# The SSD decode step with state rows on partitions: outer product and output on TensorE, one pass each on GpSimd and VectorE

## The chip, the cores and the metric

One core of one Trainium2 chip. The metric is the device time in microseconds (us) of one execution; the time of a kernel is the median of its runs. Names of engines: PE is TensorE's matmuls, PEld its weight loads, DVE is VectorE, ACT is ScalarE, POOL is GpSimd, SP issues DMAs.

## What is computed

One inference step of a two-layer decoder trunk for 1024 prompt tokens and 8 decode tokens (8 sequences, one new token each). Layer 0 is a hybrid of gated DeltaNet and retention, layer 1 is a Mamba-2 SSD mixer; a squared-ReLU MLP stands behind each. The change is in the SSD mixer's decode step: for each of 8 sequences and 32 heads (4 groups of 8) with state size 128 and head size 64

```
S_new = S * exp(g) + outer(B, x * dt)      # [state 128, head 64]
y     = C^T S_new                          # per head, 64 values
```

where `g = dt * a`, B and C belong to the group, and `S_new` is an output of its own (4 x 8 tiles of 256 KB).

## The kernel before

Activations lie with features on the partitions and the 1032 tokens along the row. The projections are exact in float32: weights and activations are split into a high and a low part in the rounded type float32r, and each product is three matmuls of 344 columns (L150, L151, L152). A weight tile comes by DMA from SP into `raw`, is scaled by the norm's weights on GpSimd (L140), rounded by ScalarE to `whi` (L144), and its rest `wlo` is made by VectorE (L145).

The SSD mixer (`ssm_mixers`, L1441) goes through 4 groups. Each group has 6 projection tiles for x, B and C (evicted by VectorE at L1451 as `sxc`, then the convolution L408 to L413 and a SiLU at L420 and L421) and 4 gate tiles (`z`, L1476, L1487). `ssd_group` (L1569) handles the 1024 prompt tokens in 4 units of 2 chunks: transposes to tokens on partitions (L1598), `xdt` (L1600), scores `sc` (L1613), decay products (L1621) that need the banks which `xdt` and `sc` free, and then L1648 to L1666 for outputs and running state. The projection tiles of the next group and the gates of the one before are interleaved with it by generators, and so is the decode step:

```
            yield
            for _ in range(2 if u == 0 else 1):
                next(dec)
                yield
```

`ssd_decode` (L1674) first makes small tables and fetches states, then takes one pair of sequences per unit. The order in which each engine finally gets its instructions is set by the tile scheduler, which mixes these streams; each engine works through its list strictly in order. PSUM has three banks for projections (`pg`), three for small products (`pm`), taken in turn. Eight buffers of [128, 512] (`half`) are shared in turn by `xdt`, `xd2`, `yi`, and the decode step's `dS` and `dpr`.

In the decode step before, a state tile `dS` [128, 4 x 128] has the features (of head pairs) on the partitions and the 128 state rows along the row. TensorE only broadcasts rows of B and C over the partitions (L1718). Per state, ScalarE scales the four quarters by exp(g) (four L1725), VectorE adds B times x dt to each quarter (four L1727), GpSimd issues the store (L1728) and multiplies by C into `dpr` (L1730), and VectorE sums `dpr` over the state rows (L1731). The other mixer's decode step has states in the other layout and does products of states with two columns (L966), a scaling on GpSimd (L979), an outer product (L1021) and an add on VectorE (L981).

Of the kernel before, what the change touches and what calls it, by code (L numbers as in the profile page):

```python
# [10 lines left out]
F32 = mybir.dt.float32  # L11
# [8 lines left out]
T = 1032                     # 1024 prompt tokens, then 8 decode tokens  # L20
# [24 lines left out]
# order of the hybrid projection's m-tiles (first column of each)  # L45
# [14 lines left out]
# blocks of the output projections: the first packed column's k-tile, the mixer outputs  # L60
# [13 lines left out]
# columns of the retention's constants  # L74
# [9 lines left out]
class Pools:  # L84
    """A mixer's two pools: what the output projection's first block needs or reuses, and the rest."""
# [10 lines left out]
class Kern:  # L96
# [35 lines left out]
    def load_w(self, src, n, normw=None, lo_eng=None, dst=None, norm_eng=None):  # L132
        """src [128, n] of a packed weight unit -> exact float32r high and low parts."""
# [73 lines left out]
    def gemm_flush(self, src, parts, evict):  # L207
        """A block of k-tiles into all 8 m-tiles; src(m) the packed weights [128, 128 * k-tiles]."""
# [16 lines left out]
    def split_piece(self, m, n, src, ssq, tp):  # L225
        """src [128, 344] fp32 becomes the residual's piece (m, n); its squares go to ssq."""
# [16 lines left out]
    def rsqrt(self, out, src):  # L243
        """out = (src) ** -0.5 for a small tile."""
# [7 lines left out]
    def rstd_from(self):  # L252
        """rstd_bc[:, t] = (sum_p ssq[p, t] / 1024 + eps) ** -0.5 on every partition; ssq lies where rstd_bc does."""
# [42 lines left out]
    def load_x(self, gp):  # L296
        """The tokens, as exact parts; their rstd; and the narrow projection, not yet scaled by it."""
# [25 lines left out]
        def square(m):  # L323
            """x[m]'s squares; those of four tiles are added up."""
# [49 lines left out]
    def softplus(self, out, x, tp, tag, bufs=None):  # L374
        """log1p(exp(x)) = max(x, 0) + 2 atanh(u / (2 + u)), u = exp(-|x|)."""
# [40 lines left out]
    def silu2(self, x, scale, tp):  # L416
        """x (1 + tanh(scale x)) in place, in two halves."""
# [39 lines left out]
    def load_mixed(self, k, raw, hi, lo):  # L457
        """A spilled mixer output [128, 1024] and its decode columns, as exact parts."""
# [7 lines left out]
    def out_first(self, name, c0, parts, stage):  # L466
        """The first k-tiles of an output projection, with the residual, go to memory."""
# [12 lines left out]
    def hyb_mixers(self, gp):  # L480
# [34 lines left out]
        def ret(t, rr, vv, gg):  # L515
            for i in range(2):
# [3 lines left out]
                for q in range(4):          # the halves of each head's features change places  # L520
# [25 lines left out]
        def step():  # L546
            """Emits a sixth of a projection (and the end of the one before)."""
# [6 lines left out]
        def project(n):  # L554
            """Emits the projections up to tile n."""
# [6 lines left out]
        def weave(mix, need, rate):  # L562
            """Emits a mixer's pieces with `rate` sixths of a projection after each."""
# [16 lines left out]
        # the output projection's first block fills in while the last mixers finish  # L580
# [22 lines left out]
    def gdn_setup(self, gp, ba):  # L603
# [14 lines left out]
        gnh = gp.tile([P, 5], F32, name="gnh")     # norm weights of the gated outputs, halved  # L618
# [4 lines left out]
        # beta and decay: [8, T] -> token-major [128, 9, 8]  # L623
# [35 lines left out]
        # rows of the cumulated decay, as exact float32r parts stacked on the contraction  # L659
# [19 lines left out]
    def gdn_head(self, gp, h, feat, st):  # L679
# [21 lines left out]
        for bi in range(2):  # L701
# [33 lines left out]
            # decay, transposed: DT[j, c, i] = exp(min(G_i - G_j, mask))  # L735
# [1150 lines left out]
```

## Time and profile before

| | |
|---|---|
| runs | 3256.97, 3253.94, 3255.11 us; median 3255.11 |
| profiled execution, span of the trace | 3239.5 us (its time outside the span is not recorded; the median is 15.6 us above the span) |
| TensorE busy | 3086.4 us, 95% |
| VectorE, ScalarE, GpSimd busy | 1740.3 (54%), 896.2 (28%), 1241.3 (38%) |
| granted TensorE clock, mean | 0.960 of full speed |
| moved by DMA | 202.13 MB, mean 62 GB/s |

Busy times are shares of the whole span, so an engine that looks idle there can be the late one in a single stage. Matmuls overlap each other, so the mean length of one is larger than the step from one to the next; the step is read from counts in a stretch where TensorE never idles.

### The profile page before, as it was taken

To read this page: it belongs to the slowest core of one execution; us is meant where nothing else is said; L and a number is where in the kernel's file an instruction comes from. 1 tells how busy PE (TensorE), PEld (TensorE's weight loads), DVE (VectorE), ACT (ScalarE), POOL (GpSimd) and SP (SyncE) were. 2 spreads that over 40 slices of the span, in tenths; PEclk is the share of its full clock that TensorE was granted. 3 is DMA by queue.
4 is the path that set the end of the run, shared out by engine and by line. 5 is a ranking of instruction groups with operands and counts; after the bars stand their busy time and mean duration, and the time that the engine had idled before them with its cause. 6 is when DMAs were issued, how large, how long until landed. Compare 5 with 4: busy or idle time off the path is not lost. (4 is left out here: it accounts for less than half of the span.)

```text
span 3239.5 us, 49390 instructions
## 1 busy us (share of the span) xinstructions
PE 3086.4 (95%) x19566; PEld 2929.6 (90%) x19566; DVE 1740.3 (54%) x3201; ACT 896.2 (28%) x1828; POOL 1241.3 (38%) x1234
## 2 busy tenths in 40 slices
PE   7989998989999999999999999999899999999998
PEld 6888888879999999999987788887899999999998
DVE  7664667464333333337886785967635333333334
ACT  3222221223111111114444444354213111111112
POOL 4232324155333323225355555444625332332324
PEclk9899999889999999999998898998899999999999
DMA  3011103142111111111111111222431111111112
GB/s 123 20 47 54 47 26 112 55 168 64 46 46 47 49 46 46 48 48 40 55 56 58 69 62 43 82 69 79 157 140 43 46 47 49 46 46 50 46 46 72
DMA packets 102326, 202.13 MB, mean 62 GB/s; under 512 B 12624, under 2 KB 27728, under 8 KB 102096
## 3 DMA queue, kind: packets, MB, share of 16 engines
q1 hardware_dynamic: 94800, 173.82, 16.7%
q0 software_dynamic: 7296, 25.17, 2.0%
q8 instruction: 154, 2.52, 0.3%
q14 instruction: 76, 0.62, 0.1%
HBM read 157.94 MB, written 38.89 MB: 61 GB/s over the span
## 5 line engine op out<-in xcount | busy, mean ns | idle before, releaser
L150 PE MATMUL pg<-xh,whi 128*128 128x344 f32 x3072 | 1020.7, 332 | 10.2 <-DVE sxc L1451 6.5
L152 PE MATMUL pg<-xh,wlo 128*128 128x344 f32 x3072 | 1012.9, 330 | 2.8 <-DVE wlo L145 2.8
L151 PE MATMUL pg<-xl,whi 128*128 128x344 f32 x3072 | 1009.0, 328 | 0.0
L150 PEld LDWEIGHTS pg<-xh,whi 128*128 128x128 f32 x3072 | 593.0, 193 | 27.7 <-issue 8.8
L152 PEld LDWEIGHTS pg<-xh,wlo 128*128 128x128 f32 x3072 | 592.8, 193 | 12.7 <-issue 5.2
L144 ACT CAST whi<-raw 128x512 fp32r<-128x512 f32 (+2 forms) x443 | 271.0, 612 | 1191.5 <-PE pg L151 723.9
L151 PEld LDWEIGHTS pg<-xl,whi 128*128 128x128 f32 x3072 | 592.3, 193 | 8.8 <-issue 5.8
L140 POOL TENSOR_TENSOR raw<-raw,vec 128x512 f32<-128x512 f32 x264 | 300.7, 1139 | 589.9 <-DMA raw<-w 339.7
L151 PE MATMUL pg<-alo,whi 128*128 128x344 f32 (+2 forms) x1476 | 472.4, 320 | 0.0
L152 PE MATMUL pg<-ahi,wlo 128*128 128x344 f32 (+2 forms) x1476 | 472.3, 320 | 0.0
L150 PE MATMUL pg<-ahi,whi 128*128 128x344 f32 (+2 forms) x1476 | 471.6, 319 | 0.0
L1236 DVE TENSOR_TENSOR acc<-acc,pg 128x344 f32<-128x344 f32 x360 | 182.8, 511 | 385.4 <-PE pg L152 385.4
L145 POOL TENSOR_TENSOR wlo<-raw,whi 128x512 fp32r<-128x512 f32 (+2 forms) x179 | 223.7, 1251 | 327.7 <-ACT whi L144 326.6
L145 DVE TENSOR_TENSOR wlo<-raw,whi 128x512 fp32r<-128x512 f32 x264 | 209.6, 794 | 193.3 <-ACT whi L144 172.2
L1227 POOL TENSOR_TENSOR r<-r 128x344 f32<-128x344 f32 x192 | 145.9, 760 | 387.6 <-ACT ahi L1226 338.5
L152 PEld LDWEIGHTS pg<-ahi,wlo 128*128 128x128 f32 x1476 | 277.6, 188 | 0.0
L150 PEld LDWEIGHTS pg<-ahi,whi 128*128 128x128 f32 x1476 | 277.5, 188 | 0.0
L151 PEld LDWEIGHTS pg<-alo,whi 128*128 128x128 f32 x1476 | 277.3, 188 | 0.0
L1228 DVE TENSOR_TENSOR alo<-r,ahi 128x344 fp32r<-128x344 f32 x192 | 135.6, 707 | 253.8 <-POOL r L1227 253.8
L1226 ACT ACTIVATE ahi<-r 128x344 fp32r<-128x344 f32 x192 | 94.5, 492 | 338.5 <-DVE r L1225 338.5
L1225 DVE SCALAR_TENSOR_TENSOR r<-pg,rstd_bc 128x344 f32<-128x344 f32 x186 | 94.8, 510 | 76.9 <-PE pg L152 75.6
L150 PE MATMUL pg<-mhi,whi 128*128 128x344 f32 x408 | 131.3, 322 | 4.1 <-DVE acc L1342 4.1
(534 smaller groups left out, 4422.9 us busy)
## 6 DMA issues: line engine op xcount, KB each, us to landing
raw<-w SPq DMA_DIRECT2D x256, 256.0 KB, 2.6
raw<-wis SPq DMA_DIRECT2D x80, 256.0 KB, 2.6
raw<-wih SPq DMA_DIRECT2D x56, 256.0 KB, 2.6
mraw<-spill SPq DMA_DIRECT2D x17, 512.0 KB, 4.1
accd<-ost SPq DMA_DIRECT2D x48, 172.0 KB, 2.1
acc<-accd SPq DMA_DIRECT2D x16, 516.0 KB, 6.9
dS<-sstate SPq DMA_DIRECT2D x32, 256.0 KB, 3.5
o_sssm<-dS POOLq DMA_DIRECT2D x32, 256.0 KB, 2.4
```

The source lines that it names most:

```text
L140: (norm_eng or nc.gpsimd).tensor_tensor(out=r3, in0=r3, in1=normw.unsqueeze(2).to_broadcast([P, k, n // k]), op=ALU.mult)
L144: nc.scalar.copy(hi[:, :n], raw[:, :n])
L145: (lo_eng or nc.vector).tensor_tensor(out=lo[:, :n], in0=raw[:, :n], in1=hi[:, :n].bitcast(F32), op=ALU.subtract)
L150: t.matmul(ps, lhsT=whi, rhs=xhi, start=start, stop=False)
L151: t.matmul(ps, lhsT=whi, rhs=xlo, start=False, stop=False)
L152: t.matmul(ps, lhsT=wlo, rhs=xhi, start=False, stop=stop)
L1225: nc.vector.scalar_tensor_tensor(out=r, in0=ps, scalar=0.0, in1=self.rstd_bc[:, s], op0=ALU.max, op1=ALU.mult)
L1226: nc.scalar.activation(hi[:, s], r, AF.Square)
L1227: nc.gpsimd.tensor_tensor(out=r, in0=r, in1=r, op=ALU.mult)
L1228: nc.vector.tensor_tensor(out=lo[:, s], in0=r, in1=hi[:, s].bitcast(F32), op=ALU.subtract)
L1236: nc.vector.tensor_tensor(out=s, in0=s, in1=ps, op=ALU.add)
```

## The change

States lie with the 128 state rows on the partitions and the 8 x 64 features of the group along the row (`pack`, `unpack`). Per group, x of the 8 decode tokens is transposed to sequences on partitions, multiplied by dt and split into exact parts in rows 0, 32 and 64 of `xr`; B likewise into `bst`. `Bm` is `bst` masked to one sequence, built for four sequences at a time on VectorE. Per state: GpSimd multiplies the tile by exp(g), TensorE makes the outer product from `Bm` and `xr` (512 columns), VectorE adds the two, GpSimd issues the store, and TensorE multiplies the four quarters of the new state with one column of C. ScalarE copies the outputs of a pair. `ssm_setup` makes exp(g) of all heads on all partitions (`segb`) once, and two zeroed tiles. Comments and docstrings are dropped throughout, which shifts the line numbers only.

```diff
@@ ssm_setup
-        sel8 = gp.tile([16, 8], F32R, name="sel8")
-        nc.vector.tensor_copy(sel8, c3[:16])
...
-        nc.tensor.transpose(pt[:32, 0:8], dt[:8, 8, :], self.ident[:8, :8])
-        nc.tensor.transpose(pt[:32, 8:16], g[:8, 8, :], self.ident[:8, :8])
-        dg = gp.tile([32, 16], F32, name="dgd")
-        nc.scalar.copy(dg, pt[:32, 0:16])
+        bg = gp.tile([8, 8, 32], F32, tag="hf", name="sbg", bufs=SHF)
...
+        nc.tensor.matmul(pt[:, 0:256], lhsT=self.ones[:8, :], rhs=bg..., start=True, stop=True)
+        egb = gp.tile([P, 8, 32], F32, name="segb")
+        nc.scalar.activation(egb..., pt[:, 0:256], AF.Exp)
+        xr = gp.tile([P, 512], F32R, name="sxr")
+        bst = gp.tile([P, 128], F32R, name="sbst")
...
@@ ssd_decode
-        for i in range(4):
-            t.matmul(pd[:, i * 16:i * 16 + 16], lhsT=selg[:32, i * 128:i * 128 + 128].bitcast(F32), rhs=st["dg"], ...)
-        a.copy(dtf, pd3[:, :, 0:8])
-        a.activation(egf, pd3[:, :, 8:16], AF.Exp)
-        v.tensor_tensor(out=xd, in0=x[:, :, dec], in1=dtf, op=ALU.mult)
-        for k, src in enumerate((B[:, dec], C[:, dec])):
-            v.tensor_copy(hi[:, k], src)
-            v.tensor_copy(parts[:, k, 0:8], hi[:, k].bitcast(F32))
-            v.tensor_tensor(out=parts[:, k, 8:16], in0=src, in1=hi[:, k].bitcast(F32), op=ALU.subtract)
...
+        for i in range(4):
+            t.transpose(pt[:8, i * 128:i * 128 + 128], x[:, i, dec], ident)
+        xd = half("dxd")[:8]
+        v.tensor_tensor(out=xd..., in0=pt[:8]..., in1=st["dt"][:8, 8, hs]..., op=ALU.mult)
+        a.copy(xr[0:8], xd)
+        a.copy(xr[32:40], xd)
+        v.tensor_tensor(out=xr[64:72], in0=xd, in1=xr[0:8].bitcast(F32), op=ALU.subtract)
+        t.transpose(pt[:8, 0:128], B[:, dec], ident)
+        a.copy(bst[0:8], pt[:8, 0:128])
+        a.copy(bst[64:72], pt[:8, 0:128])
+        v.tensor_tensor(out=bst[32:40], in0=pt[:8, 0:128], in1=bst[0:8].bitcast(F32), op=ALU.subtract)
...
         for b0 in range(0, 8, 2):
             cur, nxt = nxt, fetch(b0 + 2) if b0 < 6 else None
-            pb = self.pm()
+            if b0 % 4 == 0:
+                Bm = gp.tile([P, 4, 128], F32R, tag="dBm", name="dBm", bufs=1)
+                v.tensor_tensor(out=Bm, in0=bst..., in1=st["seq"][:, b0:b0 + 4]..., op=ALU.mult)
+            py = self.pm()
             for j in range(2):
-                t.matmul(pb[:, j * 256:j * 256 + 256], lhsT=st["sel8"][:, b0 + j:b0 + j + 1].to_broadcast([16, P]), rhs=rows, ...)
-            bc = small("bc", [P, 2, 2, 128])
-            a.copy(bc, pb.rearrange("p (b k n) -> p b k n", b=2, k=2))
-            for j in range(2):
-                b = b0 + j
-                s = cur[j].rearrange("p (i n) -> p i n", i=4)
+                b, s = b0 + j, cur[j]
+                s3 = s.rearrange("p (h k) -> p h k", h=8)
+                gs.tensor_tensor(out=s3, in0=s3, in1=st["egb"][:, b, hs]..., op=ALU.mult)
+                po = self.pm()
+                t.matmul(po, lhsT=Bm[:, b % 4], rhs=xr, start=True, stop=True)
+                v.tensor_tensor(out=s, in0=s, in1=po, op=ALU.add)
+                nc.gpsimd.dma_start(self.O["sssm"][g, b], s)
                 for i in range(4):
-                    a.activation(s[:, i], s[:, i], AF.Copy, scale=egf[:, i, b:b + 1])
-                for i in range(4):
-                    v.scalar_tensor_tensor(out=s[:, i], in0=bc[:, j, 0], scalar=xd[:, i, b:b + 1], in1=s[:, i], ...)
-                nc.gpsimd.dma_start(self.O["sssm"][g, b], cur[j])
-                pr = half("dpr").rearrange("p (i n) -> p i n", i=4)
-                gs.tensor_tensor(out=pr, in0=s, in1=bc[:, j, 1].unsqueeze(1).to_broadcast([P, 4, 128]), op=ALU.mult)
-                v.tensor_reduce(out=y[:, :, b], in_=pr, axis=AX.X, op=ALU.add)
+                    t.matmul(py[:, i * 2 + j:i * 2 + j + 1], lhsT=s[:, i * 128:i * 128 + 128], rhs=C[:, SEQ + b:SEQ + b + 1], ...)
+            a.copy(y[:, :, b0:b0 + 2], py[:, 0:8].rearrange("p (i k) -> p i k", i=4))
```

The scheduler's order changes in the SSD stage alone. Two places, both at the second pair of states of the third group, just ahead of the third unit. VectorE's list before (L1476 evicts a gate tile, L1727 works on the states, L1613 makes `sc`, L1600 `xdt`):

```order
1790 L1476 SCALAR_TENSOR_TENSOR z<-pg,rstd_bc 128x344
1791 L1727 SCALAR_TENSOR_TENSOR dS<-dbc,dxd,dS 128x128 x3
1792 L421 SCALAR_TENSOR_TENSOR z<-th,z 128x516
1793 L1727 SCALAR_TENSOR_TENSOR dS<-dbc,dxd,dS 128x128 x5
1794 L1613 TENSOR_TENSOR sc<-pm,c_67 128x256
1795 L1487 TENSOR_TENSOR z<-z 128x1032
1796 L1731 TENSOR_REDUCE dy<-dpr 128x4 x2
1797 L1555 TENSOR_SCALAR nrs<-ps 128x9
1798 L1600 TENSOR_TENSOR xdt<-pm,dt 128x512
```

Eight L1727 and two L1731 stand ahead of the first `xdt`. The same place of the changed kernel (L1482 is the eviction, L1727 now the add, L1606 `xdt`, L1718 builds `Bm`, L1619 is `sc`):

```order
1743 L1482 SCALAR_TENSOR_TENSOR z<-pg,rstd_bc 128x344
1744 L1727 TENSOR_TENSOR dS<-dS,pm 128x512
1745 L145 TENSOR_TENSOR wlo<-raw,whi 128x512
1746 L421 SCALAR_TENSOR_TENSOR z<-th,z 128x516
1747 L1727 TENSOR_TENSOR dS<-dS,pm 128x512
1748 L1606 TENSOR_TENSOR xdt<-pm,dt 128x512
1749 L1718 TENSOR_TENSOR dBm<-sbst,c_14288 128x512
1750 L1606 TENSOR_TENSOR xdt<-pm,dt 128x512
1751 L1493 TENSOR_TENSOR z<-z 128x1032
1752 L1619 TENSOR_TENSOR sc<-pm,c_67 128x256
```

Two adds have taken the place of the ten, and `xdt` has moved ahead of `sc`. TensorE's list at that place before (L1718 broadcasts B and C, L1598 and the four behind it open the unit):

```order
9808 L152 MATMUL pg<-xh_78,wlo 128x344
9809 L1718 MATMUL pm<-drows,sel_14290 128x256 x2
9810 L1598 MATMUL pm<-c_67,x 128x128 x8
9811 L1610 MATMUL pm<-c_67,bc 128x128
9812 L1611 MATMUL pm<-bc 128x128
9813 L1610 MATMUL pm<-c_67,bc 128x128
9814 L1611 MATMUL pm<-bc 128x128
9815 L150 MATMUL pg<-xh_71,whi 128x344
```

No matmul there reads a state. Now (L1726 is the outer product, L1730 the four one-column products, L1604 the transposes):

```order
9839 L1726 MATMUL pm<-sxr,dBm 128x512
9840 L150 MATMUL pg<-xh_71,whi 128x344
9841 L151 MATMUL pg<-xl_79,whi 128x344
9842 L152 MATMUL pg<-xh_71,wlo 128x344
9843 L150 MATMUL pg<-xh_72,whi 128x344
9844 L151 MATMUL pg<-xl_80,whi 128x344
9845 L152 MATMUL pg<-xh_72,wlo 128x344
9846 L150 MATMUL pg<-xh_73,whi 128x344
9847 L151 MATMUL pg<-xl_81,whi 128x344
9848 L1730 MATMUL pm<-bc,dS 128x1 x4
9849 L1726 MATMUL pm<-sxr,dBm 128x512
9850 L1604 MATMUL pm<-c_67,x 128x128 x4
```

Eight projection matmuls stand between an outer product and the products that read the new state, and the second outer product and the unit's transposes stand behind these.

## Rows read from the trace of the kernel before

**Rows 1.** The page: span, busy time of each engine, and the span in 40 equal slices (tenths busy).
```profile
span 3239.5 us, 49390 instructions
PE 3086.4 (95%) x19566; PEld 2929.6 (90%) x19566; DVE 1740.3 (54%) x3201; ACT 896.2 (28%) x1828; POOL 1241.3 (38%) x1234
...
PE   7989998989999999999999999999899999999998
...
DVE  7664667464333333337886785967635333333334
```
**Rows 2.** Windows: a plain projection stretch, and the SSD stage whole. Columns: length, busy time and count of PE, PEld, DVE, ACT, POOL; then granted clock, DMA share, GB/s.
```profile
800.00:850.00 50.00, 50.00 (x319) 50.00 (x319) 18.54 (x33) 10.99 (x20) 16.43 (x18) 1.00 0.16 47
...
1590.00:2275.00 685.00, 638.11 (x3804) 560.41 (x3804) 521.68 (x815) 313.44 (x725) 346.74 (x301) 0.91 0.19 65
```
**Rows 3.** What TensorE's matmuls waited for from 1590 to 2275 us: total us, times, longest. There are nine rows with a DVE releaser, of which the first three and the last are shown, and two with ACT.
```profile
PE pm L1621 <- DVE xdt L1600: 14.0, 8, 3.0
PE pm L1621 <- DVE sc L1613: 13.0, 5, 3.4
PE pg L150 <- DVE sxc L1451: 6.5, 4, 2.7
...
PE pm L1636 <- ACT E L1625: 1.9, 2, 0.9
...
PE pg L150 <- ACT whi L144: 1.3, 2, 0.7
...
PE pg L150 <- DVE z L1476: 1.0, 1, 1.0
```
**Rows 4.** Timeline of TensorE around one such wait: start, length, instruction, and in brackets the idle time before it and its releaser.
```profile
1997.22 0.32 PE L150 MATMUL pg<-xh,whi 128*128 128x344 f32 x1
2000.90 0.80 PE L1621 MATMUL pm<-sgrow,ssel 64*128 64x256 f32 x2 [3.36 <-DVE sc L1613]
```
**Rows 5.** Timeline of VectorE and of GpSimd ahead of that wait's end.
```profile
1993.99 0.88 DVE L1727 SCALAR_TENSOR_TENSOR dS<-dbc,dxd,dS 128x128 f32<-128x128 f32 x3 [0.53 <-ACT dbc L1720]
...
1995.39 5.12 DVE L1727 SCALAR_TENSOR_TENSOR dS<-dbc,dxd,dS 128x128 f32<-128x128 f32 x5
2000.43 0.41 DVE L1613 TENSOR_TENSOR sc<-pm,c 128x256 f32<-128x256 f32 x1
...
1995.55 2.45 POOL L1484 TENSOR_TENSOR x<-x,z 128x1032 f32<-128x1032 f32 x1 [4.18 <-DVE z L421]
...
1998.55 1.27 POOL L1730 TENSOR_TENSOR dpr<-dS,dbc 128x512 f32<-128x512 f32 x1
```
**Rows 6.** The window behind that wait, and a stretch at the low clock elsewhere (columns as in rows 2).
```profile
1714.00:1720.00 6.00, 6.00 (x20) 5.18 (x21) 3.76 (x7) 2.60 (x9) 4.58 (x5) 0.50 0.28 91
...
2000.60:2010.60 10.00, 9.70 (x36) 8.88 (x37) 3.43 (x6) 2.79 (x9) 3.67 (x3) 0.50 0.06 26
```
**Rows 7.** The decode step's groups by line and form from 1590 to 2275 us: count, busy us, mean ns, idle time before them and its releasers; and the lengths of L1727.
```profile
L1727 DVE SCALAR_TENSOR_TENSOR dS<-dbc,dxd,dS 128x128 f32<-128x128 f32 x128 | 74.1, 624 | 2.3 <-ACT dbc L1720 2.3
L1730 POOL TENSOR_TENSOR dpr<-dS,dbc 128x512 f32<-128x512 f32 x32 | 43.8, 1370 | 0.7
L1725 ACT ACTIVATE dS<-dS,degf 128x128 f32<-128x128 f32 x128 | 40.8, 389 | 49.6 <-DMA dS<-sstate 49.5
L1731 DVE TENSOR_REDUCE dy<-dpr 128x4 f32<-128x512 f32 x32 | 21.7, 677 | 4.9 <-POOL dpr L1730 4.9
L1720 ACT COPY dbc<-pm 128x512 f32<-128x512 f32 x16 | 9.3, 582 | 0.8 <-PE pm L1718 0.8
...
L1727 DVE SCALAR_TENSOR_TENSOR dS<-dbc,dxd,dS x128: 334/344/2506, 1626.2 to 2263.6; 128x128 f32<-128x128 f32 x128
```
**Rows 8.** The nearest rows for the new instructions: lengths (min/median/max ns) of the other mixer's step and of L1666, group rows of L145 and L1660 in the SSD stage, and pieces of the timeline (the weight loads of sixteen products of two columns, of two L1718 and of the transposes behind them).
```profile
L979 POOL TENSOR_TENSOR dS<-dS,deg x8: 1031/1037/1345, 492.6 to 544.8; 128x512 f32<-128x512 f32 x8
L981 DVE TENSOR_TENSOR dS<-dS,pm x8: 686/686/689, 501.4 to 549.8; 128x512 f32<-128x512 f32 x8
L1021 PE MATMUL pm<-om,oxt x12: 488/497/792, 500.9 to 651.0; 24*128 24x512 f32 x8, 48*128 48x512 f32 x4
L1666 DVE TENSOR_TENSOR S<-S,ps x28: 670/686/689, 1609.0 to 2262.4; 128x512 f32<-128x512 f32 x28
L145 DVE TENSOR_TENSOR wlo<-raw,whi 128x512 fp32r<-128x512 f32 x66 | 67.2, 1018 | 12.9 <-PE pg L152 11.8 <-ACT whi L144 0.9
L1660 PE MATMUL ps<-xd,bt 128*128 128x512 f32 x64 | 34.1, 614 | 1.7 <-DVE x L1650 1.7
491.29 1.91 PEld L966 LDWEIGHTS pm<-dkq,dS 128*128 128x128 f32 x16
1992.83 0.29 PEld L1718 LDWEIGHTS pm<-drows,sel 16*128 16x128 f32 x2 [0.22 <-issue]
1993.26 0.86 PEld L1598 LDWEIGHTS pm<-c,x 128*128 128x128 f32 x8
```
**Rows 9.** VectorE ahead of two other waits of L1621, those that end at 1678.48 and at 1782.65.
```profile
1676.31 0.67 DVE L1731 TENSOR_REDUCE dy<-dpr 128x4 f32<-128x512 f32 x1
...
1779.20 0.92 DVE L1476 SCALAR_TENSOR_TENSOR z<-pg,rstd_bc 128x344 f32<-128x344 f32 x2
```
**Rows 10.** The other mixer's decode step, with its four bursts of L966 (columns as in rows 2).
```profile
491.00:545.00 54.00, 50.55 (x328) 45.69 (x327) 41.20 (x122) 9.30 (x20) 26.97 (x29) 1.00 0.42 133
```

More of the change, by code (lines that the diff above doesn't have):

```diff
@@ L1431, in ssm_setup @@
         nc.vector.tensor_tensor(out=sel, in0=self.ident[:64, 0:32], in1=self.ident[:64, 32:64], op=ALU.add)
+        bg = gp.tile([8, 8, 32], F32, tag="hf", name="sbg", bufs=SHF)
+        nc.vector.tensor_tensor(out=bg, in0=g[:8, 8, :].unsqueeze(1).to_broadcast([8, 8, 32]),
+                                in1=self.ident[:8, :8].unsqueeze(2).to_broadcast([8, 8, 32]), op=ALU.mult)
         pt = self.pm()
-        nc.tensor.transpose(pt[:32, 0:8], dt[:8, 8, :], self.ident[:8, :8])
-        nc.tensor.transpose(pt[:32, 8:16], g[:8, 8, :], self.ident[:8, :8])
-        dg = gp.tile([32, 16], F32, name="dgd")
-        nc.scalar.copy(dg, pt[:32, 0:16])
-        st.update(dt=dt, gc=gc, kdf=kdf, egend=egend, grow=grow, sel=sel, sel8=sel8, dg=dg)
+        nc.tensor.matmul(pt[:, 0:256], lhsT=self.ones[:8, :], rhs=bg.rearrange("p b h -> p (b h)"), start=True, stop=True)
+        egb = gp.tile([P, 8, 32], F32, name="segb")
+        nc.scalar.activation(egb.rearrange("p b h -> p (b h)"), pt[:, 0:256], AF.Exp)
+        xr = gp.tile([P, 512], F32R, name="sxr")
+        bst = gp.tile([P, 128], F32R, name="sbst")
+        for r, n in ((xr, 4), (bst, 1)):
+            nc.vector.tensor_scalar(out=r.rearrange("p (c k) -> p c k", c=n), in0=self.U.unsqueeze(1).to_broadcast([P, n, 128]),
+                                    scalar1=0.0, scalar2=None, op0=ALU.mult)
+        st.update(dt=dt, gc=gc, kdf=kdf, egend=egend, grow=grow, sel=sel, seq=c3, egb=egb, xr=xr, bst=bst)
         return st
@@ L1586, in ssd_group @@
         selg = selg.rearrange("p h k -> p (h k)")
-        dec = self.ssd_decode(gp, g, x, B, C, st, half, selg)
+        dec = self.ssd_decode(gp, g, x, B, C, st, half)
         S = None
@@ L1672, in ssd_group, with ssd_decode @@
         nc.gpsimd.dma_start(self.O["pssm"][g], S)
-    def ssd_decode(self, gp, g, x, B, C, st, half, selg):
+    def ssd_decode(self, gp, g, x, B, C, st, half):
         nc = self.nc
@@ L1678, in ssd_decode @@
         ident = self.ident
+        hs = slice(g * 8, g * 8 + 8)
         dec = slice(SEQ, T)
-        def small(name, sh, dt=F32):
-            return gp.tile(sh, dt, tag="d" + name, name="d" + name, bufs=1)
-        pd = self.pm()
+        xr, bst = st["xr"], st["bst"]
+        pt = self.pm()
         for i in range(4):
-            t.matmul(pd[:, i * 16:i * 16 + 16], lhsT=selg[:32, i * 128:i * 128 + 128].bitcast(F32), rhs=st["dg"], start=True, stop=True)
-        pd3 = pd[:, 0:64].rearrange("p (i k) -> p i k", i=4)
-        dtf, egf = small("dtf", [P, 4, 8]), small("egf", [P, 4, 8])
-        a.copy(dtf, pd3[:, :, 0:8])
-        a.activation(egf, pd3[:, :, 8:16], AF.Exp)
-        xd = small("xd", [P, 4, 8])
-        v.tensor_tensor(out=xd, in0=x[:, :, dec], in1=dtf, op=ALU.mult)
-        hi, parts = small("hi", [P, 2, 8], F32R), small("parts", [P, 2, 16])
-        for k, src in enumerate((B[:, dec], C[:, dec])):
-            v.tensor_copy(hi[:, k], src)
-            v.tensor_copy(parts[:, k, 0:8], hi[:, k].bitcast(F32))
-            v.tensor_tensor(out=parts[:, k, 8:16], in0=src, in1=hi[:, k].bitcast(F32), op=ALU.subtract)
-        pt = self.pm()
-        for k in range(2):
-            t.transpose(pt[:16, k * 128:k * 128 + 128], parts[:, k], ident)
-        rows = small("rows", [16, 256], F32R)
-        a.copy(rows, pt[:16, 0:256])
-        y = small("y", [P, 4, 8])
+            t.transpose(pt[:8, i * 128:i * 128 + 128], x[:, i, dec], ident)
+        xd = half("dxd")[:8]
+        v.tensor_tensor(out=xd.rearrange("p (h k) -> p h k", h=8), in0=pt[:8].rearrange("p (h k) -> p h k", h=8),
+                        in1=st["dt"][:8, 8, hs].unsqueeze(2).to_broadcast([8, 8, 64]), op=ALU.mult)
+        a.copy(xr[0:8], xd)
+        a.copy(xr[32:40], xd)
+        v.tensor_tensor(out=xr[64:72], in0=xd, in1=xr[0:8].bitcast(F32), op=ALU.subtract)
+        pt = self.pm()
+        t.transpose(pt[:8, 0:128], B[:, dec], ident)
+        a.copy(bst[0:8], pt[:8, 0:128])
+        a.copy(bst[64:72], pt[:8, 0:128])
+        v.tensor_tensor(out=bst[32:40], in0=pt[:8, 0:128], in1=bst[0:8].bitcast(F32), op=ALU.subtract)
+        y = gp.tile([P, 4, 8], F32, tag="dy", name="dy", bufs=1)
         def fetch(b0):
@@ L1715, in ssd_decode @@
             cur, nxt = nxt, fetch(b0 + 2) if b0 < 6 else None
[L1716 to L1731 removed]
+            if b0 % 4 == 0:
+                Bm = gp.tile([P, 4, 128], F32R, tag="dBm", name="dBm", bufs=1)
+                v.tensor_tensor(out=Bm, in0=bst.bitcast(F32).unsqueeze(1).to_broadcast([P, 4, 128]),
+                                in1=st["seq"][:, b0:b0 + 4].unsqueeze(2).to_broadcast([P, 4, 128]), op=ALU.mult)
+            py = self.pm()
+            for j in range(2):
+                b, s = b0 + j, cur[j]
+                s3 = s.rearrange("p (h k) -> p h k", h=8)
+                gs.tensor_tensor(out=s3, in0=s3, in1=st["egb"][:, b, hs].unsqueeze(2).to_broadcast([P, 8, 64]), op=ALU.mult)
+                po = self.pm()
+                t.matmul(po, lhsT=Bm[:, b % 4], rhs=xr, start=True, stop=True)
+                v.tensor_tensor(out=s, in0=s, in1=po, op=ALU.add)
+                nc.gpsimd.dma_start(self.O["sssm"][g, b], s)
+                for i in range(4):
+                    t.matmul(py[:, i * 2 + j:i * 2 + j + 1], lhsT=s[:, i * 128:i * 128 + 128], rhs=C[:, SEQ + b:SEQ + b + 1], start=True, stop=True)
+            a.copy(y[:, :, b0:b0 + 2], py[:, 0:8].rearrange("p (i k) -> p i k", i=4))
             if b0 == 6:
```

8 lines of the change are left out of this document (3 added, 5 removed).

## Prediction, made before the changed kernel was run

> **What bounds the kernel now.** I read the page first. TensorE is busy for 95% of the span, everything else far less, so the question is never "which engine is faster" but "what does TensorE do, or wait for, in the stage that is changed" [rows 1]. Counting the 40 slices from 0, the SSD stage is slices 20 to 28, and there VectorE has its only 9 [rows 1]; the next view shows what TensorE does in it.
>
> Next the windows view by stretch. A pure projection stretch (800 to 850 us) has TensorE busy 50.00 of 50 at clock 1.00 and issues 319 matmuls, 0.157 us each [rows 2]. The SSD stage from 1590 to 2275 has TensorE busy 638.1 of 685 us, so 46.9 us idle, at a mean clock of 0.91, with VectorE busy 521.7 (76%) and ScalarE and GpSimd about half [rows 2]. Since the clock has two levels, 1.2 and 2.4 GHz, a mean of 0.91 over 685 us means about 121 us at the lower one.
>
> Then the waits of TensorE in that stage: 43.5 of the 46.9 us are waits for VectorE (nine rows whose releaser is DVE, the first 14.0, the last 1.0), 27.0 of them for `xdt` and `sc` at the start of a unit, in 13 waits of up to 3.4 us [rows 3]. The timeline shows one: after L150 at 1997.22 TensorE stands for 3.36 us until VectorE has made `sc` [rows 4]. VectorE was in five L1727 instructions of the decode step, 5.12 us for what takes 0.344 us each alone, because GpSimd ran L1484 and L1730 at that time [rows 5]. After that wait the clock is at 0.50 for the next 10 us shown, which hold 36 matmuls instead of 64 [rows 6]. In the plain stretch at 1714 to 1720 it is 20 in 6 us, 0.300 us each [rows 6]. So a microsecond at the low clock loses 1 - 0.157/0.300 = 0.48 us, and 121 us lose 58. **The stage is TensorE-bound with two leaks, 47 us idle and 58 us of clock, and both open behind VectorE.**
>
> **The change part by part.**
>
> *VectorE.* Removed: 128 L1727, 74.1 us (0.624 mean, 0.344 median, up to 2.5), 32 L1731, 21.7 us, and about 5 us of small pieces: 101 us [rows 7]. Added: 32 adds of state and PSUM; the nearest row is the other mixer's same step, L981, 0.686 us at minimum and median, 0.689 at most: 22.0 us. And 8 builds of `Bm` [128 x 512] by a product from SBUF, nearest row L145 in this stage, 1.018: 8 us, with 3 us of set-up [rows 8]. Net 101 - 33 = -68 us of 522. The piece of the order shows it: before the wait of [rows 4], eight L1727 stand ahead of `sc`; now two adds, and `xdt` comes first.
>
> *ScalarE.* 128 L1725 (40.8 us) and 16 L1720 (9.3) go, 50 us [rows 7]; some 3 us of copies come. ScalarE is busy 313 of 685 us [rows 2], and TensorE waits for it 3.2 us in all [rows 3]; I count nothing.
>
> *GpSimd.* 32 L1730 at 1.37 us become 32 multiplies; the nearest row is L979, 1.04 us median [rows 7, 8]: -10 us, counted at nothing, being 51% busy [rows 2]. What is new is a wait: ScalarE waited 49.5 us for states to land [rows 7], now GpSimd would, with weight scalings (L140) queued behind. Bounds 0 to 49.5; I take 0: a unit takes eight of the shared half tiles (four `xdt` and `xd2`, two `yi`, two `dS`) where with `dpr` it took ten, and there are eight buffers, so a fetch finds the buffer of the pair before it free a unit ahead. The 32 fetches and 32 stores of 256 KB stay.
>
> *TensorE, work.* Added: 32 outer products of 512 columns; by L150's 0.157 us for 344 columns that is 0.234 each, 7.5 us; the upper bound is L1660's full-float product of 512 columns, 0.614 us if nothing overlapped, 20 us [rows 8]. I take the lower, because the new operands have the rounded float type of L150. Then 128 products of one column; nearest row L966, 16 products of two columns with the same 128 x 128 state as weights in 1.91 us, 0.119 each: 15.3 us. 20 transposes at 0.86/8 = 0.11: 2.2 us [rows 8]. Removed: 32 L1718, 0.43 us for two (1992.83 to 1993.26), 6.9 us [rows 8], and 40 small products of the set-up at 0.11, 4.4 us. **Net +14 us** (up to +26), all on the path.
>
> *TensorE, waits that go.* In two of the three waits whose VectorE queues I read (1676 and 1997), decode work stands ahead; in the third (1779) it is the evictions of a gate tile, L1476 [rows 5, 9]. At 1997 the decode work ahead is 6.0 us and two adds are 1.4, so the 4.6 us saved exceed the 3.36 us of the wait; not every wait will be covered like that. Two thirds of 43.5 is 29, nine tenths of it **-26** (bounds 0 and -43.5). Late next, where a wait goes, is the gate's or the convolution's own VectorE work.
>
> *TensorE, waits that come.* This is the price of the change. Before, no matmul of the decode step depended on a state. Now `py` stands in TensorE's queue and waits for VectorE's add, which waits for GpSimd's pass and the outer product, and everything behind `py` on TensorE, the projections, waits with it. On VectorE the evictions, the weight splits and the convolution are queued behind the add; on GpSimd the store, and L140 behind it. The order puts 8 projection matmuls between outer product and `py`: 0.234 + 8 x 0.157 = 1.49 us. Needed are L1021's 0.49 us of a 512-column product and 0.69 of an add, 1.18 us [rows 8]. So 0.3 us to spare if VectorE is free, and 0.5 to 1 us short if one eviction or weight split is in front. I take 0.25 us per state, **+8** (bounds 0, and 2.1 us, the mean of today's waits at L1621, 27.0/13: +67).
>
> *The clock.* 121 us at the low level follow some 13 long waits [rows 3, 6]. If half the time goes with the waits: 60 x 0.48 = **-29** (bounds 0 and -58). The other mixer's decode step shows whether bursts of one- and two-column products pull it down: 491 to 545 us holds four bursts of 16, with 3.4 us idle, at 1.00 [rows 10]. There is a rule that speaks against me. The Trainium skill, "TensorE: Matmul & The Clock Gate", section "A second HAM failure mode: psum-queue depth-cycling", says that frequent short idling of TensorE between groups of matmuls makes the clock swing between its levels; by it the new `py` waits, which cycle the three `pm` banks, would make this term a loss. [rows 10] does not bear it out for short idling and [rows 4, 6] show a fall after one long wait, so I give it a small chance below.
>
> **Sum.** 14 - 26 + 8 - 29 = -33 us. The profiled execution's span is 3239.5, which would become 3206.5; the 15.6 us between span and median I leave as they are, so 3255.1 - 33 = **3222**.
>
> **The rivals.**
>
> 1. *The add is late, and TensorE waits for each state* (slower). Place: every `py`, 32 times. For it: VectorE is busy 76%, and its own evictions already hold TensorE up (6.5 us before L150 [rows 3]). Against: the order leaves room, and the add reads PSUM and shows no spread in L981 or L1666 [rows 8], so GpSimd does not stretch it. At 1.0 us per state, about an eviction and half a weight split in front of each add, and no recovery of the clock: 14 - 26 + 32 = +20, 3275. Without the clock term it decides from (26 - 14)/32 = 0.4 us per state, with it from 1.3.
> 2. *Short waits keep the clock low* (slower). If each of the 16 pairs brought a fall like today's (121/13 = 9.3 us at the low level, 4.5 us lost): +71 in place of -29, so 14 - 26 + 8 + 71 = +67, 3322. (It is the rule of the Trainium skill named above.)
> 3. *Both leaks close.* All waits with decode in front go and four fifths of the clock comes back: 14 - 35 + 4 - 46 = -63, 3192. For it: the falls follow long waits. Against: 1779 waits without decode.
> 4. *No change.* The waits only move to the next late VectorE result, 14 - 14 = 0, 3255. For it: the order places L1621 straight behind the transposes, so a wait there remains.
>
> **How the numbers follow.** Forecast 0.48, its own range 3205 to 3240 (from -15 to -50). Rival 1 0.18, rival 2 0.04, rival 3 0.17, rival 4 0.13. The range reaches through rival 3 to 3188 and through rival 1 to 3278; about 0.2 is left out. A measurement of this kernel can tell 0.2%, 6.5 us, from no change. Faster: 0.48 + 0.17 = 0.65. Within: 0.13. Slower: 0.22.
>
> **What would show it.** In the stage's window: VectorE's busy time near 450; waits of TensorE for `xdt` and `sc` near 10 us instead of 27; clock near 0.95; waits before the one-column products under 10 us. If those waits sum to over 30 us, or the clock is at 0.91 still, I am wrong in the terms for new waits or for the clock; if VectorE's relief is there and the waits at L1621 are not shorter, in the term for the waits that go.

## The result, and the profile after

| | before | after | ratio, 95% interval |
|---|---|---|---|
| first comparison, 5 runs each | 3254.33 | 3237.18 (3229.36 to 3242.22) | 0.9941 [0.9922, 0.9960] |
| second, 21 and 6 runs | 3252.71 | 3229.02 (3216.45 to 3241.48) | 0.9933 [0.9908, 0.9959] |
| third, 17 and 6 runs | 3250.99 | 3222.05 (3217.31 to 3246.88) | 0.9918 [0.9887, 0.9949] |

The change makes the kernel faster, by 17, 24 and 29 us in the three comparisons; over all runs of the two kernels (71 and 17) the means are 3252.8 and 3229.7, 23 us apart. The forecast was -33, with 3205 to 3240 as its own range: the sign was right, and so was the place of the gain. One term of the sum was half of what it should have been, and two others gave back more than was forecast, so that the total is close partly by luck.

The page of the changed kernel answers to [rows 1]:

```profile
span 3235.4 us, 49609 instructions
...
PE 3103.6 (96%) x19802; PEld 2953.0 (91%) x19802; DVE 1686.0 (52%) x3067; ACT 859.2 (27%) x1704; POOL 1238.5 (38%) x1234
...
DVE  7574757555433333335787676766635333333334
```

The span is only 4 us shorter, although VectorE has lost its 9. Part of that is the choice of the execution: every later run is 1.8 us longer than its span (3237.18 and 3235.4 here), so the 15.6 us that were taken as time outside the span are mostly not that. The trace of the kernel before is of an execution that was some 13 us quicker than its median. Where the rest went shows when both kernels are cut at the same work. Both issue 15600 projection products of 344 columns. Up to the 7250th, TensorE's lists are the same (the layer ahead of the SSD stage); from there to the 10250th lies the stage. The windows view cut at these marks, for the kernel before (columns as in [rows 2]):

```profile
1514.50:2311.50 797.00, 740.00 (x4425) 659.66 (x4425) 611.31 (x956) 350.80 (x784) 387.83 (x340) 0.91 0.20 68
0.00:1514.50 1514.50, 1440.01 (x9416) 1367.34 (x9417) 769.72 (x1596) 360.09 (x709) 534.74 (x580) 0.97 0.19 60
```

For the changed kernel, with the stage's window of [rows 2] for comparison:

```profile
1543.30:2309.10 765.80, 731.81 (x4662) 660.28 (x4661) 556.36 (x821) 311.54 (x660) 383.97 (x340) 0.96 0.21 71
1590.00:2275.00 685.00, 659.21 (x4229) 590.99 (x4229) 496.40 (x722) 285.02 (x616) 353.71 (x313) 0.97 0.20 69
0.00:1543.30 1543.30, 1467.11 (x9415) 1392.07 (x9416) 771.98 (x1597) 361.63 (x709) 535.27 (x580) 0.95 0.19 59
```

The stage is 31 us shorter, as forecast. But it begins 29 us later, after the same instructions, at a mean clock of 0.95 in place of 0.97. Windows at fixed times are not the same work any more, so from here on the marks are used.

The waits of TensorE in the changed stage answer to [rows 3] (first nine rows; L1627 is L1621 of before, L1730 reads the new states):

```profile
PE pm L1730 <- DVE dS L1727: 5.5, 4, 2.3
PE pg L150 <- DVE ost L473: 3.5, 2, 3.1
PE pg L150 <- DVE z L1482: 3.5, 2, 2.3
PE ps L1654 <- DVE E L1635: 3.5, 3, 1.5
PE pm L1642 <- ACT E L1631: 2.8, 3, 1.0
PE ps L294 <- DVE dg L292: 2.8, 6, 0.6
PE ps L1559 <- DVE z L1493: 2.8, 3, 0.9
PE ps L1654 <- DVE x L1656: 2.7, 3, 1.6
PE pm L1627 <- DVE xdt L1606: 1.5, 4, 0.5
```

27.0 us for `xdt` and `sc` have become 1.5, and the new wait for the add is 5.5. One of its four cases, TensorE first and then VectorE ahead of it:

```profile
1861.29 0.32 PE L152 MATMUL pg<-xh,wlo 128*128 128x344 f32 x1
1863.88 0.37 PE L1730 MATMUL pm<-bc,dS 128*128 128x1 f32 x1 [2.27 <-DVE dS L1727]
```
```profile
1860.38 2.72 DVE L1569 SCALAR_TENSOR_TENSOR x<-x,vec,ps 128x512 f32<-128x512 f32 x4 [0.51 <-PE ps L294]
1863.02 0.21 DVE L1573 SCALAR_TENSOR_TENSOR dmix<-x,vec,ps 128x8 f32<-128x8 f32 x1
1863.15 0.68 DVE L1727 TENSOR_TENSOR dS<-dS,pm 128x512 f32<-128x512 f32 x1
```

Four results of the norm stood ahead of the add: this is rival 1, at two places instead of 32.

The decode step's instructions in the stage, by tile (lengths min/median/max in ns; forms behind the span of starts), then who waited for them, and TensorE's new groups by line:

```profile
L1730 PE MATMUL pm<-bc,dS x256: 164/250/373, 1656.2 to 2258.1; 128*128 128x1 f32 x128
L1724 POOL TENSOR_TENSOR dS<-dS,segb x32: 1036/1238/2022, 1642.0 to 2225.2; 128x512 f32<-128x512 f32 x32
L1727 DVE TENSOR_TENSOR dS<-dS,pm x32: 672/679/689, 1655.5 to 2255.6; 128x512 f32<-128x512 f32 x32
...
  ACT dy L1731: 78.4, 16
  POOL o_sssm L1728: 22.4, 13
```
```profile
L1730 PE MATMUL pm<-bc,dS 128*128 128x1 f32 x256 | 34.8, 256 | 5.5 <-DVE dS L1727 5.5
...
L1726 PE MATMUL pm<-sxr,dBm 128*128 128x512 f32 x32 | 14.6, 456 | 0.2 <-ACT th L420 0.2
```

The first row of the tile view is the one to stop at: it counts 256 records (x256; the x128 at its end is how many of them the view sampled for their form), but the program issues 128 of these products, four for each of 32 states. The weight loads of one state's four products say the same; the timeline lists eight:

```profile
1656.23 0.97 PEld L1730 LDWEIGHTS pm<-bc,dS 128*128 128x128 f32 x8 [0.20 <-DVE dS L1727]
```

A full-float product is two passes, each with its own weight load. The add's 0.68 us is as forecast, and ScalarE's 78.4 us of waiting to copy outputs delays nobody on TensorE's list (no `dy` among its waits, of which the nine longest stand above).

### The profile page after: what moved, and what is told of

It is laid out like the page before. It is cut to its first block, busy times and chain, and to the rows that moved or that the text cites. A ratio compares the mean times of both kernels' runs of the same rounds, so it can differ in the third digit from the quotient of the medians.

```text
span 3235.4 us, 49609 instructions
## 1 busy us (share of the span) xinstructions
PE 3103.6 (96%) x19802; PEld 2953.0 (91%) x19802; DVE 1686.0 (52%) x3067; ACT 859.2 (27%) x1704; POOL 1238.5 (38%) x1234
## 5 line engine op out<-in xcount | busy, mean ns | idle before, releaser
L140 POOL TENSOR_TENSOR raw<-raw,vec 128x512 f32<-128x512 f32 x264 | 294.1, 1114 | 607.9 <-DMA raw<-w 335.6
L145 POOL TENSOR_TENSOR wlo<-raw,whi 128x512 fp32r<-128x512 f32 (+2 forms) x179 | 226.5, 1266 | 330.3 <-ACT whi L144 330.1
L145 DVE TENSOR_TENSOR wlo<-raw,whi 128x512 fp32r<-128x512 f32 x264 | 201.6, 764 | 184.9 <-ACT whi L144 177.7
```

Source lines behind the costliest of these rows:

```text
L140: (norm_eng or nc.gpsimd).tensor_tensor(out=r3, in0=r3, in1=normw.unsqueeze(2).to_broadcast([P, k, n // k]), op=ALU.mult)
L145: (lo_eng or nc.vector).tensor_tensor(out=lo[:, :n], in0=raw[:, :n], in1=hi[:, :n].bitcast(F32), op=ALU.subtract)
```

## The experiments

Every profiled run is cut at the two marks. Idle is the window's length less TensorE's busy time; the time at 1.2 GHz is from the clock's records in the trace; the rest is stage less idle less 0.48 of the low time (the price of a low microsecond worked out ahead of the run), so it stands for TensorE's work at full speed. All in us.

| kernel | first mark | stage | idle | low clock | rest | VectorE busy |
|---|---|---|---|---|---|---|
| before | 1514.5 | 797.0 | 57.0 | 136.5 | 674.5 | 611.3 |
| before_again | 1533.9 | 792.0 | 59.5 | 119.5 | 675.1 | 614.1 |
| after | 1543.3 | 765.8 | 34.0 | 58.0 | 704.0 | 556.4 |
| after_again | 1548.1 | 761.0 | 33.5 | 47.8 | 704.6 | 555.3 |
| after_third | 1521.2 | 770.1 | 33.6 | 68.3 | 703.7 | 556.4 |
| before_less_dve | 1538.5 | 734.0 | 38.8 | 34.1 | 678.8 | 535.5 |
| after_dve_load | 1535.1 | 788.1 | 44.0 | 95.6 | 698.2 | 603.1 |
| after_no_py | 1539.7 | 733.6 | 33.6 | 51.2 | 675.4 | 557.8 |
| after_py_double | 1535.9 | 805.5 | 32.4 | 88.7 | 730.5 | 554.1 |
| after_py_late | 1540.5 | 759.5 | 31.6 | 54.6 | 701.7 | 556.7 |
| late_py_double | 1526.8 | 804.6 | 29.6 | 92.2 | 730.7 | 557.7 |
| after_bm_act | 1541.0 | 760.3 | 34.9 | 41.0 | 705.7 | 544.4 |
| late_bm_act | 1540.6 | 757.1 | 30.2 | 51.2 | 702.3 | 543.0 |

The rest is the same to 1 us for the same kernel, so 0.48 fits traces that differ in clock alone. Between kernels the split is good to some 5 us only: before_less_dve has the TensorE instructions of before and comes out 4 above it, after_dve_load those of after and comes out 6 below. Part of this is low time in which TensorE stood idle and lost nothing by it; with the low time taken only while TensorE is busy, the rest is 677.0 and 677.5 before, 704.3 to 705.0 after, 679.1 and 702.7 in these two runs.

**Is the late start of the stage the change's doing?** Theory: chance of the clock. Both kernels again, unchanged.

before_again: 

> The kernel before, unchanged, for a second trace. Marks: the start of the 7250th and of the 10250th projection product of 344 columns, between which the SSD stage lies; in the first traces they lie 797.0 us apart before and 765.8 after, and the first comes at 1514.5 before and 1543.3 after although both kernels have the same instructions on TensorE up to there. Theory (the difference ahead of the stage is chance of the clock): the stage is 797 within 5, and the first mark can lie anywhere from 1512 to 1545. Rival (the change itself slows what comes ahead): the first mark is within 3 of 1514.5.

after_again: 

> The changed kernel, unchanged, for a second trace. Theory (chance of the clock ahead of the stage): the stage is 766 within 6, the first mark lies anywhere from 1512 to 1545, and the whole time follows the first mark. Rival (the change slows what comes ahead): the first mark lies again at 1540 or later.

after_third: 

> The changed kernel, unchanged, beside the two others for their comparison: the stage at 761 to 766 again, the whole at 3229 to 3237, the first mark anywhere from 1512 to 1550.

The kernel before, taken again, reached the first mark 19 us later than the first time:

```profile
0.00:1533.90 1533.90, 1460.13 (x9415) 1384.95 (x9416) 771.83 (x1596) 360.13 (x709) 535.72 (x580) 0.95 0.19 59
1533.90:2325.90 792.00, 732.47 (x4426) 652.71 (x4425) 614.09 (x956) 351.18 (x784) 388.67 (x340) 0.92 0.20 68
```

The second trace of the changed kernel, at 1548.1, was what the rival expected; the third was at 1521.2:

```profile
0.00:1521.20 1521.20, 1446.28 (x9415) 1373.57 (x9416) 770.85 (x1597) 360.17 (x709) 534.19 (x580) 0.96 0.18 60
1521.20:2291.30 770.10, 736.47 (x4662) 663.85 (x4661) 556.37 (x821) 311.12 (x660) 383.87 (x340) 0.96 0.20 70
```

So one kernel alone spreads over 19 or 27 us there, and the two overlap. The low time ahead of the first mark goes from 99.0 us (before) to 170.7 (after_again), and 33.6 us of time for 71.7 us of low clock is 0.47 each, the price again. The low time explains the late start; whether the change has a part in that low time is open. The whole gained 23 us over all runs and the stage 29, and a few us ahead of the stage can't be excluded by five traces. The stage itself, 792 to 797 and 761 to 770, does not overlap (770 is 4 above what was expected of it, for 10 us more of low clock; that kernel's whole, 3222.05, fell below the expected 3229 to 3237).

**Does VectorE's load make the waits?** Taken away in the kernel before (GpSimd clears `y` instead, once for each group):

```diff
-                for i in range(4):
-                    v.scalar_tensor_tensor(out=s[:, i], in0=bc[:, j, 0], scalar=xd[:, i, b:b + 1], in1=s[:, i], ...)
...
-                v.tensor_reduce(out=y[:, :, b], in_=pr, axis=AX.X, op=ALU.add)
```

> The kernel before without the 128 L1727 (the outer product's add) and the 32 L1731 (the sum over the state rows): 96 us less on VectorE, TensorE's instructions the same. Left out: the added outer product and the output of the step. Theory (VectorE's load held TensorE up, and the long waits brought the low clock): TensorE's waits in the stage fall from 47 us to 25 or less, the time at the low clock from 123 us to under 70, and the stage takes 745 to 775 in place of 797, the whole 3205 to 3235. Rival (the change gained by another order of the lists, not by the load): the stage takes 787 to 797, the whole over 3244.

Put back in the changed kernel:

```diff
                 v.tensor_tensor(out=s, in0=s, in1=po, op=ALU.add)
...
+                for _ in range(3):
+                    v.tensor_reduce(out=dum, in_=s.rearrange("p (i n) -> p i n", i=4), axis=AX.X, op=ALU.add)
```

> The changed kernel with three idle sums over the new state on VectorE per state, behind the add: 96 x 0.67 = 65 us put back on VectorE, all else the same. Theory (the relief of VectorE pays for the change): waits and low clock come back, the stage takes 790 to 815 in place of 766, the whole 3255 to 3285. Rival (order, not load): the stage takes 762 to 772, the whole 3225 to 3245.

Taken away, the kernel before took 3198.23 us, 0.9836 [0.9815, 0.9858]; idle fell by 19 us (to 39, not to the 25 expected) and low clock by 94. The stage and the whole came out below their expected ranges, at 734.0 and 3198. The stage's window and its first four waits:

```profile
1538.50:2272.50 734.00, 695.23 (x4424) 623.73 (x4424) 535.52 (x796) 349.83 (x784) 388.25 (x343) 0.98 0.22 74
```
```profile
PE pm L1636 <- ACT E L1625: 8.7, 6, 2.0
PE ps L278 <- DVE x L1563: 4.9, 2, 2.7
PE pg L150 <- DVE z L1476: 4.4, 1, 4.4
PE pm L1621 <- DVE xdt L1600: 4.0, 4, 1.2
```

`xdt`, 14.0 before, is down to 4.0, and the largest sum is now for ScalarE. But the edit did not take away load alone: the scheduler placed the rest anew. TensorE has the same instructions in another order, and on VectorE `xdt` now stands ahead of `sc` in 16 of 16 units, as in the changed kernel, where it was 8 of 16 before. At the place where the list of the kernel before had `sc` first:

```profile
1984.52 0.69 DVE L1600 TENSOR_TENSOR xdt<-pm,dt 128x512 f32<-128x512 f32 x1 [0.50 <-PE pm L1598]
...
1986.37 0.68 DVE L1600 TENSOR_TENSOR xdt<-pm,dt 128x512 f32<-128x512 f32 x1
1986.97 0.41 DVE L1613 TENSOR_TENSOR sc<-pm,c 128x256 f32<-128x256 f32 x1
```

Put back, the changed kernel took 3253.11 us, 0.9997 [0.9981, 1.0013] of before: the whole gain was gone, 2 us short of what was expected. Its first four waits:

```profile
PE pm L1627 <- ACT E L1631: 8.3, 8, 1.4
PE pg L152 <- DVE wlo L145: 7.6, 3, 6.2
PE pm L1733 <- DVE dS L1728: 5.0, 3, 2.4
PE pm L1627 <- DVE xdt L1606: 3.7, 6, 1.3
```

The rival wanted 787 to 797 and 762 to 772 and got 734.0 and 788.1. The first figure does not speak against it, since the order changed there too; the second does, as `xdt` still stands ahead of `sc` in all 16 units and the stage is 22 us longer all the same. But with VectorE at 603 us, near its old load, idle is 44 and not 58, low clock 96 and not 128, and the old waits for `xdt` and `sc` (27.0) are at 3.7. The added sums bring back 10 of 25 us of idle time and 38 of 70 of low clock; the other part may be the order in which `xdt` stands ahead. So it is shown that VectorE's work for the decode step, by its length and by the order that the scheduler makes of it, held TensorE up. How the two share the gain is open: both runs changed both, and the sums stand at another place than the old work.

**What does a one-column product cost?** Left out (with the copies of the outputs; `y` is cleared instead), and doubled (two diffs):

```diff
...
-                for i in range(4):
-                    t.matmul(py[:, i * 2 + j:i * 2 + j + 1], lhsT=s[:, i * 128:i * 128 + 128], rhs=C[:, SEQ + b:SEQ + b + 1], ...)
-            a.copy(y[:, :, b0:b0 + 2], py[:, 0:8].rearrange("p (i k) -> p i k", i=4))
...
```
```diff
+                    t.matmul(py[:, 8 + i * 2 + j:8 + i * 2 + j + 1], lhsT=s[:, i * 128:i * 128 + 128], rhs=C[:, SEQ + b:SEQ + b + 1], ...)
```

after_no_py: 

> The changed kernel without the 128 one-column products of the new states (output of the step left out). Marks as before; the changed kernel's stage takes 761 to 766. If a product of one column costs what the prediction took, 0.119 us, the stage loses 15 us: 746 to 751. If each is two passes of 0.11 to 0.12 us (the trace lists 256 of them), it loses 30: 730 to 737. If they also bring waits that lower the clock, more than 40: under 725.

after_py_double: 

> The changed kernel with each of the 128 one-column products done twice, the second into other columns of the same bank: no new dependence, only TensorE's work. At 0.119 us each the stage takes 15 us more, 776 to 781; as two passes each 30 us more, 791 to 796.

Without them 3200.91 us, 0.9813 [0.9749, 0.9878], and the stage is 733.6:

```profile
1539.70:2273.30 733.60, 699.99 (x4405) 628.67 (x4404) 557.79 (x821) 310.23 (x644) 383.61 (x343) 0.97 0.22 74
```

The rest falls by 28.7 us from the changed kernel's mean of 704.1, 0.224 us a product, and idle and clock stay: two passes each. Doubled, the rest rises by 26.4 (0.206 each), but the stage by 40, to 805.5, more than either expected range: low clock went from 58 to 89 us while idle did not move. The whole took 3264.49, 1.0024 [0.9989, 1.0058].

**Is it the wait ahead of the bursts, or the bursts?** A burst is the run of one-column products of a pair of states. A pair's products issued a unit later, single and double (`outs` holds the products and the copy of a pair):

```diff
+        def outs(p0, S):
...
         for b0 in range(0, 8, 2):
+            if b0:
+                outs(b0 - 2, old)
             cur, nxt = nxt, fetch(b0 + 2) if b0 < 6 else None
...
```

after_py_late: 

> The changed kernel with the one-column products of a pair issued a unit later (72 to 144 projection products behind the outer product, where it was 3 to 10 in most pairs), the last pair's aside. If the waits for the add and the falls of the clock behind them cost something (5.5 us of waits, some 20 us at the low clock, at 0.48), the stage takes 748 to 757 in place of 761 to 766. If they are no cost of their own, it stays within 761 to 766.

late_py_double: 

> The one-column products a unit later and each done twice: TensorE's work as in the run that doubled them (some 30 us more than the changed kernel), but nothing waits for the add. In that run the time at the low clock in the stage rose from 48 to 58 us to 89, though the waits stayed at 32 us. If the long bursts of one-column products themselves bring the clock down, it is 80 to 95 us here too and the stage takes 800 to 806. If it was the waits ahead of the bursts, it is 50 to 65 us, and the stage takes 785 to 792.

Later, no one-column product waits any more, but `sc` is waited for instead, and the transposes (L1604) wait for the add. Idle is 31.6 in place of 33.7, and the stage (759.5) lies between the two expected ranges, 1.5 us under the unchanged kernel's spread. The edit moved the wait more than it took it away, so what the 5.5 us cost by themselves is not shown. The first two waits:

```profile
PE pm L1627 <- DVE sc L1619: 6.7, 3, 2.2
PE pm L1604 <- DVE dS L1734: 3.0, 2, 1.5
```

Later and doubled, no one-column product waits either (the transposes do, twice), and the low clock is still 92 us, with idle at 29.6: the bursts do it. (3263.98 us, 1.0038 [1.0019, 1.0058].)

```profile
PE pm L1604 <- DVE dS L1735: 2.8, 2, 1.4
```

Of its 15 falls of the clock in the stage, 13 have no step over 0.6 us between TensorE's starts in the 5 us ahead. Eleven of these come within a burst of one-column products or at most 1.3 us behind it; the other two come 2.2 and 1.0 us behind a burst of four-column products, the sums of the norm; the first of these bursts:

```profile
1823.68 2.07 PE L1559 MATMUL ps<-ones_r,z 128*128 128x4 f32 x18
```

One of the eleven: the first and last products of a pair's burst, 8 products each done twice (L1715, L1716), and then the window ahead of it, the burst, and what came behind:

```profile
1710.42 0.32 PE L152 MATMUL pg<-xh,wlo 128*128 128x344 f32 x1
1710.58 0.28 PE L1715 MATMUL pm<-bc,dS 128*128 128x1 f32 x2
...
1713.85 0.36 PE L1716 MATMUL pm<-bc,dS 128*128 128x1 f32 x2
1714.07 0.71 PE L1734 MATMUL pm<-sxr,dBm 128*128 128x512 f32 x2
```
```profile
1706.50:1710.50 4.00, 4.00 (x27) 4.00 (x27) 1.63 (x3) 0.00 (x0) 4.00 (x4) 1.00 0.21 80
1710.50:1714.10 3.60, 3.60 (x35) 3.60 (x33) 0.52 (x1) 0.62 (x1) 1.45 (x3) 1.00 0.06 13
1715.20:1718.60 3.40, 3.40 (x16) 2.97 (x14) 2.34 (x6) 2.18 (x5) 2.37 (x3) 0.51 0.49 164
```

TensorE is busy throughout these three windows, and the clock halves behind the burst. In the changed kernel as it stands the bursts are at most half as long, and there each of the 26 falls in the stages of its three traces has a step of over 1.2 us close ahead of it or across it; in late_bm_act one fall comes within such a burst with no step over 0.5 us ahead.

**Is there more to take?** VectorE's masked B by ScalarE, alone and with the later products:

```diff
-                v.tensor_tensor(out=Bm, in0=bst..., in1=st["seq"][:, b0:b0 + 4]..., op=ALU.mult)
+                for k in range(4):
+                    a.activation(Bm[:, k], bst.bitcast(F32), AF.Copy, scale=st["seq"][:, b0 + k:b0 + k + 1])
```

after_bm_act: 

> The changed kernel with the masked B made by ScalarE (four scaled copies of 128 columns in place of one VectorE product of 512): 11 us less on VectorE, 12 to 15 more on ScalarE, which is busy 42% of the stage. By what VectorE's load was worth in the two runs that changed it (22 to 27 us for 62 us added, 55 to 63 for 85 to 96 taken away) 4 to 7 us less: the stage takes 755 to 761. Rival (the builds lie where nothing waits for VectorE): 761 to 766.

late_bm_act: 

> Both edits that went the right way together: the one-column products a unit later, the masked B by ScalarE. Alone the stage took 759.5 and 760.2 us in place of 761 to 766. If the two add, 753 to 758, the whole 6 to 8 us below the changed kernel. Rival (both were chance): 760 to 766, the whole within 3 us of it.

Some 12 us came off VectorE, and the stages of 760.3 and 757.1, both within the ranges expected, are 1 to 4 us below the unchanged kernel's shortest. The whole, 3222.52 beside 3222.05 for the unchanged one, is not the 6 to 8 us lower that was expected and shows no gain: if there is one, the clock's spread ahead of the stage (1521 to 1548 for the unchanged kernel) can hide it. Alone the edit gave 3228.93.

## Why the prediction was right, and where it was off

Means of the stage, two traces before and three after: 794.5 to 765.6, -28.9 us. Forecast -33.

- *VectorE's load.* -57 us between the marks, forecast -68. The adds took 0.68 us each as forecast; `Bm` took 1.43 us a build where 1.02 was assumed, and some old work became longer beside it (the gates' sums, L1487 before and L1493 now, 18.9 to 25.6 us for 12). "Near 450" in the old window came out as 496, part of that because the window holds other work now. The direction carried.
- *Waits that go and come*: forecast -26 + 8 = -18. Idle fell from 58.3 to 33.7, **-24.6**. `xdt` and `sc` fell from 27.0 to 1.5 us, more than the two thirds assumed; 5.5 of the 8 us at L1730 came, though as two waits of over 2 us and not as 0.25 for each state.
- *The clock*: forecast -29. Low time fell from 128.0 to 58.0 us, 70.0 x 0.48 = **-34**.
- *TensorE's work*: forecast +14, bounds +14 to +26. It is **+29** (704.1 - 674.8), and 24 to 28 where the low time is taken only while TensorE is busy: near or above its upper bound, and some twice the forecast. This is the step that failed, by its size: the price of a one-column product. The row of L966 in [rows 8] has 16 weight loads in 1.91 us, and I took them for 16 products; the burst has 8 instructions there, each listed twice (so the four bursts of [rows 10] are of 8 products too). So the price of a product was 0.24, not 0.12 us, and 128 of them 30, not 15; leaving them out gave back 28.7. The outer products, 512 columns at a median step of 0.31 us where 0.234 was taken, together with the transposes roughly take up what the change removes. The Trainium skill, "FP8 and Floating Point Precision", section "TensorE Precision Notes", gives true float32 four passes; the trace disagrees with it, 256 records for 128 products.

-24.6 - 34 + 29 = -29 (the last is what the split leaves, so the sum must close): two gains larger than forecast by 12 us cover a cost that was larger by 15. That the total of the stage came so close to -33 is luck.

- *GpSimd's wait for the states* was set to 0, and was: L1724 has no idle time before it in this stage. Its passes took 1.30 us in the mean, not 1.04, which cost nothing that the waits show:

```profile
L1724 POOL TENSOR_TENSOR dS<-dS,segb 128x512 f32<-128x512 f32 x32 | 40.9, 1303 | 0.0
```

- *Rival 1* happened where four norm results stood ahead of the add, and moving the products away from there gained under 2 us beyond the spread: other waits, for `sc` and of the transposes for the add, took its place.
- *Rival 2* did not come: the low clock halved. But it has a neighbour, bursts that bring the clock down without a wait, which the prediction argued away with [rows 10]: bursts of 8 products in two passes did not show it there, and those of the changed kernel do not show it either. Done twice, the bursts went with 31 to 34 us more of low clock, 15 to 16 us of time; without waits ahead of them this is shown by late_py_double, while in after_py_double some of the falls follow waits for the add. The rule that the prediction names from the Trainium skill, "TensorE: Matmul & The Clock Gate", section "A second HAM failure mode: psum-queue depth-cycling", speaks of idling between groups; 13 of the 15 falls in late_py_double had none ahead, so the trace shows a fall that the rule does not cover.
- *Why the first comparison gave only -17*, 3 us inside the edge of the range: the stage is shorter in every trace, by 22 to 36 us from one trace to another, but the low clock ahead of the stage, where TensorE's lists are the same, changes from one execution to the next (99.0 us low in the first trace of before, 116.1 to 170.7 in the three after), and the medians of five runs carry that chance. The prediction set what a measurement can tell at 0.2%; its three runs of before lay within 3 us, but 21 later ones lie between 3233.17 and 3262.14, and 18 more between 3241.59 and 3285.92.

## What to carry to other kernels

Read the number of instructions from the program and the number of records from the trace before dividing one by the other: a full-float product of one column is listed, and paid, as two passes, 0.11 us each here, as much as a transpose of 128 columns ([rows 8]). When a busy TensorE waits for another engine, look at what stands in that engine's queue ahead of the result; work moved from there to TensorE can pay even when TensorE is the bound, because idle time and low clock can fall together (here by 25 and 70 us). An edit that is meant to change load alone may change the order too: compare the lists of the two runs before saying which of them did it. Compare two traces at the same work, not at the same time, and split a stage into work, idle time and low clock before explaining its length.

## What the runs showed of the hardware that was not expected

- A float32 product of one column with 128 x 128 weights costs 0.21 to 0.22 us in two passes; eight loads for four products took 0.97 us.
- The granted clock fell to 1.2 GHz behind doubled bursts of one-column products with TensorE busy throughout (3.60 of 3.60 us), and 13 of 15 falls in that run had no step over 0.6 us in the 5 us ahead. In the kernel before, each of its 14 and 12 falls in the stages of its two traces had a step of over 1 us close ahead of it or across it.
- The same 7250 projection products, with the same instructions around them, took 1514.5 to 1548.1 us in 13 traces, with 99.0 to 170.7 us of them at the low clock; a straight line in the low time fits all 13 to 4 us.
